# Cross attention of a streaming encoder step: half of the cached keys turned on VectorE, half on TensorE

## The chip, the cores and the metric

One Trainium2 chip, one core. The metric is device microseconds of one execution of the whole program. A profile is one execution more, recorded instruction by instruction, and times inside it count from the start of its span.

## What is computed

A two-layer encoder step. Each layer is a mixer, a cross attention and a SwiGLU, over 512 frames of one new stream (the prompt) and 16 frames of each of 8 running streams (the samples). Only the cross attention matters here:

```python
def cross_attn(h, mk, mv, w_q, w_o):
    b, t, _ = h.shape
    q = (h @ w_q).reshape(b, t, X_HEADS, X_HEAD_DIM)
    s = jnp.einsum('bqhd,bkhd->bhqk', q, mk).astype(jnp.float32) * X_SCALE
    p = jax.nn.softmax(s, axis=-1).astype(mv.dtype)
    o = jnp.einsum('bhqk,bkhd->bqhd', p, mv).reshape(b, t, X_WIDTH)
    return o @ w_o
```

There are 4 heads of 256 dimensions and 256 memory tokens. For the prompt, keys and values come from `mem_prompt` and were written to device memory earlier in the program (`kvd`). For the 8 samples they are inputs, `cache_mem_k` and `cache_mem_v` of shape (2, 8, 256, 4, 256).

## The kernel before

Every product with a weight is made of fp32 values split in two parts, hi and lo, and three passes (hi by hi, hi by lo, lo by hi). `load_w` fetches a weight in units of 1024 columns (`raw`, two buffers), and `split_unit` (L142) splits each: hi on ScalarE (L150), lo on VectorE (L151), three buffers of each part.

`cross_phase` runs once per layer. It first makes the queries of heads 0 and 1 (`q_list`, L840), then merges three lists of steps four times (L1035 to L1038): `sample_list(pr, bq)` for a pair of heads and four samples, `prompt_list(h)` for one head of the prompt, and either the queries of a later head or a part of the output projection. The merged stretches are called stages 1 to 4 here.

- `q_list`: per head four products of 320 columns (two halves `dt` of the head's 256 dimensions, two halves of the 640 frames), each 24 matmuls at L204 whose stationary side is 128 columns of the weight. Each `dt` has a weight unit of its own (all 8 blocks of 128 rows by 128 columns).
- `sample_list`: `keys` (L947) turns one key, the 256 by 256 block of one head of one sample: four transposes on TensorE into PSUM (L956), and one copy to `KT`, on VectorE for every second sample (L960, `b % 2 == 0`), on ScalarE for the others (L962). There are 32 keys a layer, 8 a stage. `load_key` asks for a key three keys ahead, one DMA of 256 KB into one of four `kr` buffers (L941). After 8 keys follow `scores` (L969), the softmax, `trans` (L978), `values` (L992, with `vr` from L985) and `turn` (L1002).
- `prompt_list`: `load` asks for the head's keys and values (`kv`, one buffer, L884), `keys` turns the keys (L891), then twice scores (L218), softmax, `trans` (L915) and values (L218).

The program's text is not yet the order of the work: a scheduler in the layer below puts the instructions of each engine in order, each engine then runs its own in that order, and they wait for each other by semaphores. All the DMAs here go through SP's one queue, in order.

The forgetting attention (`fox_phase`) already has the kind of step that the change brings: its cached keys are loaded by four DMAs of 32 partitions each (L684) and turned by VectorE in blocks of 32 by 32 (L692).

Of the kernel before, what the change touches and what calls it, by code (L numbers as in the profile page):

```python
# [9 lines left out]
F32 = mybir.dt.float32  # L10
# [8 lines left out]
P = 128  # L19
D = 1024  # L20
KD = D // P
# [71 lines left out]
def fox_mla_kernel(ctx: ExitStack, tc: tile.TileContext, I, O):  # L93
# [72 lines left out]
    def load_w(cols, k0=0, kt=KD, per=4):  # L166
        parts = []
        n = max(c1 for _, c1, _ in cols)
        k = 0
        while k < kt:  # L170
            m = min(per, kt - k)
            srcs = []
            for c0, c1, src in cols:
                sv = src[(k0 + k) * P:(k0 + k + m) * P, :].rearrange("(k p) n -> p k n", p=P)
                srcs.append((c0, c1, sv))
            hi, lo = split_unit(srcs, m, n)
            parts.append((m, hi, lo))
            k += m
        return Weight(parts)
# [3 lines left out]
    def ws_ops(w, wc, acts, ac, kt):  # L183
        return [(w.get(wi, k)[:, wc], acts[ai][:, k, ac]) for wi, ai in PASSES for k in range(kt)]
# [643 lines left out]

    def cross_phase(l, nx, rest):
        w_q, w_o = I["w_x_q"][l], I["w_x_o"][l]  # L830
        mk = I["cache_mem_k"][l].rearrange("b (m p) h d -> p (b m) (h d)", p=P)
        mv = I["cache_mem_v"][l].rearrange("b (m p) h d -> p (b m) (h d)", p=P)
        with tc.tile_pool(name=f"x{l}", bufs=2, reuse_waits="tile") as xp:
            AHEAD = 3
# [5 lines left out]
            def q_list(h):  # L840
                Q = Qps[h // 2]
                L = []
                d = {}

                def load(dt):
                    if dt == 0:
                        qs_[h] = [xp.tile([P, 2, NP], F32R, tag=f"qT{i}", name=f"qT{i}", bufs=2) for i in range(2)]
                    c0 = h * XD + dt * P
                    d[dt] = load_w([(0, P, w_q[:, c0:c0 + P])], per=8)

                def done(ps, dt, half):
                    qT = qs_[h]
                    n = HALF if half == 0 else NP - HALF
                    hs = slice(half * HALF, half * HALF + n)
                    evac_split(qT[0][:, dt, hs], qT[1][:, dt, hs], ps[:, 0:n], X_SCALE)
                    if half == 1:
                        o = TS * (h % 2)
                        A.activation(Q[:, 2 * (h % 2) + dt, :, o:o + TS],
                                     ps[:, n:HALF].rearrange("p (b t) -> p b t", t=TS), AF.Copy, scale=X_SCALE)

                for half in range(2):
                    for dt in range(2):
                        if half == 0:
                            L.append(lambda dt=dt: load(dt))
                        L += gemm(lambda dt=dt, half=half: ws_ops(d[dt], slice(0, P), nx.T,
                                                                  slice(half * HALF, (half + 1) * HALF), KD),
                                  HALF, lambda ps, dt=dt, half=half: done(ps, dt, half), parts=3)
                return L

            def softmax(pw, sp):  # L870
                nm = small.tile([P, 1], F32, tag="nm", name="nm")
# [2 lines left out]
                A.activation(pw, sp[:, 0:NMEM], AF.Exp, bias=nm, accum_out=ss)  # L874
                softmax_tail(pw, ss, NMEM)

            def prompt_list(h):
                d = {}

                def load():  # L880
                    kv = npool.tile([P, 2, 2, XD], F32, tag="gb", name="kv", bufs=1)
                    d["kv"] = [kv[:, i] for i in range(2)]
                    for i in range(2):
                        S.dma_start(kv[:, i], kvd[l][i].rearrange("(t p) n -> p t n", p=P)[:, :, h * XD:(h + 1) * XD])  # L884

                def keys():
                    d["kT"] = [xp.tile([P, 2, NMEM], F32R, tag=f"kT{i}", name=f"kT{i}", bufs=1) for i in range(2)]
                    pt = psum_t()
                    for dt in range(2):
                        for mt in range(2):  # L890
                            T.transpose(out=pt[:, dt * NMEM + mt * P:dt * NMEM + (mt + 1) * P],  # L891
                                        in_=d["kv"][0][:, mt, dt * P:(dt + 1) * P], identity=ident)
                    evac_split(d["kT"][0], d["kT"][1], pt.rearrange("p (d m) -> p d m", m=NMEM))
                    d["v"] = [xp.tile([P, 2, XD], F32R, tag=f"v{i}", name=f"v{i}", bufs=1) for i in range(2)]
                    evac_split(d["v"][0], d["v"][1], d["kv"][1])
                    oTp[h] = [xp.tile([P, 2, NP], F32R, tag=f"oT{i}", name=f"oT{i}", bufs=3) for i in range(2)]

                def scores(q2):
                    buf = npool.tile([P, D], F32, tag="hn", name="hn", bufs=2)
                    d["pw"] = [buf[:, j * NMEM:(j + 1) * NMEM] for j in range(2)]  # L900
                    for j in range(2):
                        qc = slice((2 * q2 + j) * P, (2 * q2 + j + 1) * P)
                        sp = psum_s()
                        for dt in range(2):
                            mm3(sp[:, 0:NMEM], [q[:, dt, qc] for q in qs_[h]], [k[:, dt, :] for k in d["kT"]],
                                start=(dt == 0), stop=(dt == 1))
                        softmax(d["pw"][j], sp)

                def trans():
                    d["PT"] = [xp.tile([P, 2, 256], F32R, tag=f"PT{i}", name=f"PT{i}", bufs=1) for i in range(2)]  # L910
                    pt = psum_t()
                    for mt in range(2):
                        for j in range(2):
                            i = 2 * mt + j
                            T.transpose(out=pt[:, i * P:(i + 1) * P], in_=d["pw"][j][:, mt * P:(mt + 1) * P],  # L915
                                        identity=ident)
                    evac_split(d["PT"][0], d["PT"][1], pt.rearrange("p (m q) -> p m q", q=256))

                def values(q2):
                    op = psum_o()  # L920
                    for dt in range(2):
                        for mt in range(2):
                            mm3(op[:, dt * 256:(dt + 1) * 256], [v[:, mt, dt * P:(dt + 1) * P] for v in d["v"]],
                                [p_[:, mt, :] for p_ in d["PT"]], start=(mt == 0), stop=(mt == 1))
                    oc = slice(q2 * 256, (q2 + 1) * 256)
                    evac_split(oTp[h][0][:, :, oc], oTp[h][1][:, :, oc], op.rearrange("p (d q) -> p d q", q=256))

                L = [load, keys]
                for q2 in range(2):
                    L += [lambda q2=q2: scores(q2), trans, lambda q2=q2: values(q2)]  # L930
                return L
# [3 lines left out]
            def load_key(n):  # L935

                if n < 32:
                    pr, bq, hh, b = n // 16, n // 8 % 2, n // 4 % 2, n % 4
                    hc = slice((2 * pr + hh) * XD, (2 * pr + hh + 1) * XD)
                    krs[n] = xp.tile([P, 2, XD], F32, tag="kr", name="kr", bufs=4)  # L940
                    S.dma_start(krs[n], mk[:, 2 * (4 * bq + b):2 * (4 * bq + b) + 2, hc])  # L941

            def sample_list(pr, bq):
                Q = Qps[pr]
# [2 lines left out]
                def keys(hh, b):  # L947
                    n = 16 * pr + 8 * bq + 4 * hh + b
                    load_key(n + AHEAD)
                    kr = krs.pop(n)  # L950
                    if b % 2 == 0:
                        d["KT"][hh, b // 2] = xp.tile([P, 2, 2, NMEM], F32, tag="KT", name="KT", bufs=4)
                    pt = psum_t()
                    for dt in range(2):
                        for mt in range(2):
                            T.transpose(out=pt[:, dt * NMEM + mt * P:dt * NMEM + (mt + 1) * P],  # L956
                                        in_=kr[:, mt, dt * P:(dt + 1) * P], identity=ident)
                    src = pt.rearrange("p (d m) -> p d m", m=NMEM)
                    if b % 2 == 0:
                        V.tensor_copy(d["KT"][hh, b // 2][:, 0], src)  # L960
                    else:
                        A.copy(d["KT"][hh, b // 2][:, 1], src)  # L962

                def scores():
                    sp = psum_s()
# [64 lines left out]
            for n in range(AHEAD):  # L1030
                load_key(n)
            ql = q_list(0)
            for f in ql[:6] + rest[:1] + ql[6:8] + rest[1:] + ql[8:] + q_list(1):
                f()
            merge(sample_list(0, 0), prompt_list(0), q_list(2))  # L1035
            merge(sample_list(0, 1), prompt_list(1), q_list(3))
            merge(sample_list(1, 0), prompt_list(2), out_steps(0))
# [757 lines left out]
```

## Time and profile before

| | us |
|---|---|
| median of 3 runs | 2092.14 |
| lowest and highest run | 2087.58, 2093.4 |
| the profiled execution, its own time | 2091.71 |
| its span in the trace | 2089.9 |
| mean granted clock of TensorE | 0.996 of full speed |

The span is the time from the first to the last instruction. "PE" is TensorE's matmuls, "PEld" its loads of the stationary side, which overlap matmuls; DVE is VectorE, ACT ScalarE, POOL GpSimd, SP the engine that issues the DMAs. L204 is line 204 of the kernel.

### The profile page before, as it was taken

How to read it: one execution, taken by the hardware profiler on the slowest of the kernel's cores; microseconds unless marked ns; L12 is line 12 of the kernel's file. 1: busy time of each engine (PE TensorE's matmuls, PEld its weight loads, DVE VectorE, ACT ScalarE, POOL GpSimd, SP SyncE). 2: the span in 40 equal slices, each digit the busy share in tenths (PEclk: the TensorE clock that was granted, in tenths of full speed). 3: DMA queues.
4: the chain of work that ended last, by engine and by line, in shares of the span. 5: the costliest groups of instructions: out<-in, count | busy, mean ns of one | idle time of the engine just before them, and what ended most of it. 6: DMA issues, size and time to landing. Idle time of an engine off the chain costs nothing. (4 is left out here: it accounts for less than half of the span.)

```text
span 2089.9 us, 34810 instructions
## 1 busy us (share of the span) xinstructions
PE 2034.7 (97%) x13629; PEld 1817.9 (87%) x13629; DVE 1390.8 (67%) x2658; ACT 888.0 (42%) x1723; POOL 195.2 (9%) x398
## 2 busy tenths in 40 slices
PE   7999999999999999999999989999999999999998
PEld 7988888777987899999998978887987899999996
DVE  5455555655556896687677567777556896686686
ACT  4434444544443443343344455554443443343342
POOL 1222222210000000000002301101000000000000
PEclk9999999999999999999999999999999999999999
DMA  7565655477464322232222342113463322232221
GB/s 194 119 160 124 148 135 142 146 243 229 151 197 133 100 88 74 81 91 71 81 82 64 96 109 52 53 51 102 149 196 131 101 81 75 80 99 71 81 81 61
DMA packets 334203, 236.37 MB, mean 113 GB/s; under 512 B 99140, under 2 KB 298564, under 8 KB 334040
## 3 DMA queue, kind: packets, MB, share of 16 engines
q1 hardware_dynamic: 334040, 234.15, 38.8%
q8 instruction: 108, 1.77, 0.4%
q14 instruction: 55, 0.45, 0.1%
HBM read 216.90 MB, written 17.21 MB: 112 GB/s over the span
## 5 line engine op out<-in xcount | busy, mean ns | idle before, releaser
L204 PE MATMUL mm<-hT,whi 128*128 128x320 f32 x1744 | 287.5, 311 | 2.9 <-ACT hT L222 2.9
L151 DVE TENSOR_TENSOR wlo<-raw,whi 128x1024 fp32r<-128x1024 f32 (+4 forms) x145 | 169.8, 1174 | 156.5 <-ACT whi L150 116.5
L204 PEld LDWEIGHTS mm<-hT,whi 128*128 128x128 f32 x1744 | 261.0, 188 | 6.8 <-ACT hT L222 4.3
L332 DVE TENSOR_TENSOR X<-mm,X 128x512 f32<-128x512 f32 x270 | 183.5, 687 | 119.7 <-PE mm L204 118.1
L150 ACT CAST whi<-raw 128x1024 fp32r<-128x1024 f32 (+4 forms) x145 | 144.8, 1003 | 146.7 <-PE mm L204 74.9
L204 PE MATMUL mm<-whi,oT 128*128 128x512 f32 x544 | 180.3, 407 | 3.8 <-DVE X L332 2.2
L1136 ACT CAST whi<-tw 128x512 fp32r<-128x512 f32 (+1 forms) x120 | 91.9, 766 | 213.7 <-PE mm L204 127.4
L204 PE MATMUL mm<-whi,aT 128*128 128x512 f32 x560 | 173.0, 390 | 1.2 <-ACT aT L1101 1.2
L204 PE MATMUL mm<-hT,wlo 128*128 128x320 f32 x872 | 156.7, 312 | 0.0
L204 PEld LDWEIGHTS mm<-hT,wlo 128*128 128x128 f32 x872 | 133.3, 188 | 3.3 <-issue 3.2
L232 POOL TENSOR_SCALAR rstd<-ss 128x1 f32<-128x1 f32 x49 | 16.2, 330 | 1265.4 <-ACT hn L230 1261.0
L204 PE MATMUL mm<-s,whi 128*128 128x320 f32 x768 | 128.2, 309 | 0.0
L204 PE MATMUL mm<-whi,hT 128*128 128x256 f32 (+2 forms) x800 | 125.5, 295 | 0.3 <-ACT whi L150 0.3
L204 PEld LDWEIGHTS mm<-whi,aT 128*128 128x128 f32 x560 | 104.4, 188 | 23.5 <-ACT aT L1101 2.0
L204 PEld LDWEIGHTS mm<-whi,oT 128*128 128x128 f32 x544 | 96.7, 189 | 26.2 <-DVE X L332 4.6
L204 PEld LDWEIGHTS mm<-s,whi 128*128 128x128 f32 x768 | 116.6, 188 | 0.0
L1137 DVE TENSOR_TENSOR wlo<-tw,whi 128x512 fp32r<-128x512 f32 (+1 forms) x120 | 103.5, 862 | 19.1 <-ACT whi L1136 17.4
L204 PEld LDWEIGHTS mm<-whi,hT 128*128 128x128 f32 x800 | 109.1, 191 | 3.8 <-issue 1.7
L204 PE MATMUL mm<-wlo,oT 128*128 128x512 f32 x272 | 109.0, 401 | 0.0
L204 PE MATMUL mm<-wlo,aT 128*128 128x512 f32 x280 | 108.8, 389 | 0.0
L1136 ACT CAST whi<-raw 128x1024 fp32r<-128x1024 f32 x44 | 46.3, 1052 | 131.7 <-PE mm L204 71.0
L204 PE MATMUL ps_s<-whi,aT 128*128 128x512 f32 x320 | 98.6, 389 | 0.0
(336 smaller groups left out, 4199.4 us busy)
## 6 DMA issues: line engine op xcount, KB each, us to landing
rawg<-w_ffn_gu SPq DMA_DIRECT2D x80, 512.0 KB, 3.8
raw<-w_ffn_down SPq DMA_DIRECT2D x44, 512.0 KB, 3.7
raw<-w_x_kv SPq DMA_DIRECT2D x32, 512.0 KB, 4.4
kr<-cache_mem_k SPq DMA_DIRECT2D x64, 256.0 KB, 4.8
vr<-cache_mem_v SPq DMA_DIRECT2D x32, 512.0 KB, 6.1
raw<-w_fox_in SPq DMA_DIRECT2D x30, 512.0 KB, 6.5
kr<-cache_fox_k SPq DMA_DIRECT2D x64, 128.0 KB, 5.1
vr<-cache_fox_v SPq DMA_DIRECT2D x16, 512.0 KB, 5.2
```

The source lines that it names most:

```text
L150: A.copy(hi[:, 0:m], raw[:, 0:m])
L151: V.tensor_tensor(lo[:, 0:m], raw[:, 0:m], hi[:, 0:m].bitcast(F32), ALU.subtract)
L204: T.matmul(st["ps"][:, 0:n], lhsT=l, rhs=r, start=(j == 0), stop=(j == m - 1))
L232: G.tensor_scalar(r, ss, EPS, None, ALU.add)
L332: V.tensor_tensor(xs, ps, xs, ALU.add)
L1136: A.copy(hi[:, o:o + m], src)
L1137: V.tensor_tensor(lo[:, o:o + m], src, hi[:, o:o + m].bitcast(F32), ALU.subtract)
```

## The change

For every second sample (`b % 2 == 0`, 16 keys a layer) the key is loaded as 32 partitions by 8 by 64 numbers, by four DMAs of 64 KB in runs of 256 bytes, and `V.transpose` turns it in blocks of 32 by 32 straight into `KT`; the four transposes on TensorE and VectorE's copy out of PSUM go. In this layout the two halves of a head's dimensions are the even and the odd ones. So the other keys' transposes, those of the prompt's keys and the query product take every second column as the stationary side, and a head's query weight comes in two units of 4 blocks by 256 columns, both asked for ahead of the head's first product. `load_kv` asks for the prompt's keys and values of a head right behind the turning of the head before.

```diff
     def cross_phase(l, nx, rest):
...
-        mk = I["cache_mem_k"][l].rearrange("b (m p) h d -> p (b m) (h d)", p=P)
+        mkp = I["cache_mem_k"][l].rearrange("b (m p) h d -> p (b m) (h d)", p=P)
+        mk = I["cache_mem_k"][l].rearrange("b (m j) h d -> b j m (h d)", j=32)
...
-                def load(dt):
...
-                    c0 = h * XD + dt * P
-                    d[dt] = load_w([(0, P, w_q[:, c0:c0 + P])], per=8)
+                def load():
+                    qs_[h] = [xp.tile([P, 2, NP], F32R, tag=f"qT{i}", name=f"qT{i}", bufs=2) for i in range(2)]
+                    d["w"] = load_w([(0, XD, w_q[:, h * XD:(h + 1) * XD])])
+
+                def ops(dt, half):
+
+                    hs = slice(half * HALF, (half + 1) * HALF)
+                    return [(d["w"].get(wi, k).rearrange("p (n t) -> p t n", t=2)[:, dt], nx.T[ai][:, k, hs])
+                            for wi, ai in PASSES for k in range(KD)]
...
+            def fill_keys(r, src, h):
+
+                for g in range(4):
+                    c0 = h * XD + 64 * g
+                    S.dma_start(r[32 * g:32 * g + 32], src[:, :, c0:c0 + 64])
+
+            def turn_keys(dst, r):
+                V.transpose(dst, r.rearrange("p m (i t) -> p t m i", t=2))
...
             def prompt_list(h):
...
                 def keys():
+                    d["kv"] = kvs.pop(h)
...
-                                        in_=d["kv"][0][:, mt, dt * P:(dt + 1) * P], identity=ident)
+                                        in_=d["kv"][0][:, mt].rearrange("p (n t) -> p t n", t=2)[:, dt], identity=ident)
...
-                L = [load, keys]
+                L = [keys, lambda: load_kv(h + 1)]
...
-                    krs[n] = xp.tile([P, 2, XD], F32, tag="kr", name="kr", bufs=4)
-                    S.dma_start(krs[n], mk[:, 2 * (4 * bq + b):2 * (4 * bq + b) + 2, hc])
+                    if b % 2 == 0:
+                        krs[n] = xp.tile([P, 8, 64], F32, tag="kr", name="kr", bufs=4)
+                        fill_keys(krs[n], mk[4 * bq + b], 2 * pr + hh)
+                    else:
+                        hc = slice((2 * pr + hh) * XD, (2 * pr + hh + 1) * XD)
+                        krs[n] = xp.tile([P, 2, XD], F32, tag="kr", name="kr", bufs=4)
+                        S.dma_start(krs[n], mkp[:, 2 * (4 * bq + b):2 * (4 * bq + b) + 2, hc])
...
                     if b % 2 == 0:
                         d["KT"][hh, b // 2] = xp.tile([P, 2, 2, NMEM], F32, tag="KT", name="KT", bufs=4)
+                        turn_keys(d["KT"][hh, b // 2][:, 0], kr)
+                        return
                     pt = psum_t()
...
-                                        in_=kr[:, mt, dt * P:(dt + 1) * P], identity=ident)
-                    src = pt.rearrange("p (d m) -> p d m", m=NMEM)
-                    if b % 2 == 0:
-                        V.tensor_copy(d["KT"][hh, b // 2][:, 0], src)
-                    else:
-                        A.copy(d["KT"][hh, b // 2][:, 1], src)
+                                        in_=kr[:, mt].rearrange("p (n t) -> p t n", t=2)[:, dt], identity=ident)
+                    A.copy(d["KT"][hh, b // 2][:, 1], pt.rearrange("p (d m) -> p d m", m=NMEM))
...
+            load_kv(0)
             merge(sample_list(0, 0), prompt_list(0), q_list(2))
```

The scheduler then orders the engines anew. TensorE at the start of stage 1 of the first layer before (kr and kv are raw keys, hT the activations, whi and wlo the weight's parts):

```order
L204 MATMUL mm<-hT_6091,wlo 128x320 x4
L956 MATMUL ps_t<-cst,kr 128x128 x8
L204 MATMUL mm<-hT_6090,whi 128x320 x4
L204 MATMUL mm<-hT_6091,whi 128x320 x4
L956 MATMUL ps_t<-cst,kr 128x128 x4
L204 MATMUL mm<-hT_6092,whi 128x320 x4
```

and with the change (L906 turns the prompt's keys, L977 the samples'):

```order
L204 MATMUL mm<-hT_6091,wlo 128x320 x4
L906 MATMUL ps_t<-cst,kv 128x128 x4
L977 MATMUL ps_t<-cst,kr 128x128 x4
L204 MATMUL mm<-hT_6090,whi 128x320 x4
L204 MATMUL mm<-hT_6091,whi 128x320 x4
L204 MATMUL mm<-hT_6092,whi 128x320 x4
```

Two of the three keys that stood here are gone, and the prompt's keys stand first. TensorE behind the samples' scores of stage 1 before (pws is the softmax's result, PTs its transpose, vr the cached values):

```order
L969 MATMUL ps_s<-KT,Qp_6193 32x256 x16
L915 MATMUL ps_t<-cst,hn 128x128 x4
L204 MATMUL mm<-hT_6090,whi 128x320 x4
L204 MATMUL mm<-hT_6091,whi 128x320 x4
L204 MATMUL mm<-hT_6092,whi 128x320 x4
L204 MATMUL mm<-hT_6093,whi 128x320
L978 MATMUL ps_t<-cst,pws 128x128 x2
L204 MATMUL mm<-hT_6093,whi 128x320 x3
L204 MATMUL mm<-hT_6090,wlo 128x320
L992 MATMUL ps_o<-vr,PTs 32x256 x16
```

and with the change:

```order
L986 MATMUL ps_s<-KT,Qp_6193 32x256 x16
L204 MATMUL mm<-hT_6090,whi 128x320 x4
L204 MATMUL mm<-hT_6091,whi 128x320 x4
L930 MATMUL ps_t<-cst,hn 128x128 x4
L204 MATMUL mm<-hT_6092,whi 128x320
L995 MATMUL ps_t<-cst,pws 128x128 x2
L204 MATMUL mm<-hT_6092,whi 128x320 x3
L204 MATMUL mm<-hT_6093,whi 128x320 x4
L1009 MATMUL ps_o<-vr,PTs 32x256 x10
```

Between scores and the transpose of their softmax there stood 13 matmuls of 320 columns, and now 9; behind it 4, and now 7. SP's queue for stage 2 of the first layer before:

```order
L941 DMA kr<-cache_mem_k 128x2x256 x4
L884 DMA kv<-kvd_85 128x2x256 x2
L941 DMA kr<-cache_mem_k 128x2x256 x3
L148 DMA raw<-w_x_o 128x1024
L985 DMA vr<-cache_mem_v 128x4x256 x3
L941 DMA kr<-cache_mem_k 128x2x256
L985 DMA vr<-cache_mem_v 128x4x256
```

and with the change:

```order
L895 DMA kv<-kvd_85 128x2x256 x2
L876 DMA kr<-cache_mem_k 32x8x64 x4
L960 DMA kr<-cache_mem_k 128x2x256
L1002 DMA vr<-cache_mem_v 128x4x256
L876 DMA kr<-cache_mem_k 32x8x64 x4
L1002 DMA vr<-cache_mem_v 128x4x256
L960 DMA kr<-cache_mem_k 128x2x256
L1002 DMA vr<-cache_mem_v 128x4x256
L876 DMA kr<-cache_mem_k 32x8x64 x4
L1002 DMA vr<-cache_mem_v 128x4x256
L960 DMA kr<-cache_mem_k 128x2x256
L148 DMA raw<-w_x_o 128x1024 x2
```

Before, a stage's four DMAs of values stood together at the end of the stage ahead (the rows above hold stage 3's). Now they stand one by one among the keys of their own stage, the last of them behind four DMAs for a key of the next stage.

## Rows read from the trace of the kernel before

**Rows 1.** The page's head: the span, and busy time of each engine.
```profile
span 2089.9 us, 34810 instructions
...
PE 2034.7 (97%) x13629; PEld 1817.9 (87%) x13629; DVE 1390.8 (67%) x2658; ACT 888.0 (42%) x1723; POOL 195.2 (9%) x398
```
**Rows 2.** Busy time by stretch: stages 1 to 4, first and second layer.
```profile
core 0: us, PE busy (x) PEld busy (x) DVE busy (x) ACT busy (x) POOL busy (x), PEclk, DMA share, GB/s
557.50:676.00 118.50, 118.07 (x938) 99.47 (x940) 68.15 (x141) 49.52 (x114) 0.00 (x0) 1.00 0.52 168
1500.00:1615.00 115.00, 113.95 (x894) 95.71 (x893) 64.55 (x137) 46.16 (x108) 0.00 (x0) 1.00 0.52 169
```
**Rows 3.** Groups by line: loads of the keys' transposes; busy, mean ns | idle before.
```profile
L956 PEld LDWEIGHTS ps_t<-cst,kr 128*128 128x128 f32 x256 | 30.0, 140 | 6.1 <-DMA kr<-cache_mem_k 2.2 <-ACT KT L962 1.6 <-DVE KT L960 0.4
...
L891 PEld LDWEIGHTS ps_t<-cst,kv 128*128 128x128 f32 x32 | 3.5, 141 | 1.7 <-ACT KT L962 1.7
```
**Rows 4.** Timeline of TensorE's loads in stage 1: start, us, what.
```profile
572.85 0.51 PEld L956 LDWEIGHTS ps_t<-cst,kr 128*128 128x128 f32 x4
573.32 1.17 PEld L204 LDWEIGHTS mm<-hT,whi 128*128 128x128 f32 x8
```
**Rows 5.** Timeline of TensorE's loads ahead of stage 1, query product of head 1.
```profile
552.97 1.22 PEld L204 LDWEIGHTS mm<-hT,wlo 128*128 128x128 f32 x8
554.14 2.39 PEld L204 LDWEIGHTS mm<-hT,whi 128*128 128x128 f32 x16
556.49 1.21 PEld L204 LDWEIGHTS mm<-hT,wlo 128*128 128x128 f32 x8
```
**Rows 6.** Groups by line: VectorE's copy of a key, and its block transpose.
```profile
L960 DVE COPY KT<-ps_t 128x512 f32<-128x512 f32 x32 | 22.0, 688 | 8.1 <-PE ps_t L956 8.1
L692 DVE STREAM_TRANSPOSE KT<-kr 128x512 f32<-128x512 f32 x32 | 21.6, 693 | 0.0
```
**Rows 7.** The page's DMA issues: KB each, median us from issue to landing.
```profile
kr<-cache_mem_k SPq DMA_DIRECT2D x64, 256.0 KB, 4.8
vr<-cache_mem_v SPq DMA_DIRECT2D x32, 512.0 KB, 6.1
...
kr<-cache_fox_k SPq DMA_DIRECT2D x64, 128.0 KB, 5.1
```
**Rows 8.** Two lines' issues on SP: ns of one issue, least, median, most.
```profile
L941 SPq DMA_DIRECT2D kr<-cache_mem_k x64: 367/368/679, 515.2 to 1594.9; - x64
...
L684 SPq DMA_DIRECT2D kr<-cache_fox_k x64: 321/562/3513, 18.0 to 357.1; - x64
```
**Rows 9.** Timeline at the first layer's first query product.
```profile
527.29 2.64 PEld L204 LDWEIGHTS mm<-hT,whi 128*128 128x128 f32 x18 [1.05 <-ACT hT L222]
...
529.21 1.22 DVE L151 TENSOR_TENSOR wlo<-raw,whi 128x1024 fp32r<-128x1024 f32 x1
```
**Rows 10.** Timeline of TensorE's loads from the samples' scores to values, stage 1.
```profile
577.30 1.45 PEld L969 LDWEIGHTS ps_s<-KT,Qp 128*32 128x32 f32 x32 [0.19 <-issue]
579.16 0.42 PEld L915 LDWEIGHTS ps_t<-cst,hn 128*128 128x128 f32 x4 [0.41 <-issue]
579.55 1.92 PEld L204 LDWEIGHTS mm<-hT,whi 128*128 128x128 f32 x13
581.79 0.20 PEld L978 LDWEIGHTS ps_t<-cst,pws 128*128 128x128 f32 x2 [0.33 <-issue]
...
582.75 0.81 PEld L992 LDWEIGHTS ps_o<-vr,PTs 128*32 128x32 f32 x20 [0.19 <-ACT PTs L980]
```
**Rows 11.** Loads for matmuls of 16 columns, L457: timeline's ends, and the counts.
```profile
51.87 0.30 PEld L457 LDWEIGHTS ps_t<-pw,cst 128*128 128x128 f32 x2
...
54.10 0.45 PEld L204 LDWEIGHTS mm<-hT,wlo 128*128 128x128 f32 x3
...
L457 PEld LDWEIGHTS ps_t<-pw,ones x12: 192/192/192, 52.1 to 53.8; 128*128 128x128 f32 x12
...
L457 PEld LDWEIGHTS ps_t<-pw,cst x8: 186/192/192, 51.9 to 54.0; 128*128 128x128 f32 x8
```

More of the change, by code (lines that the diff above doesn't have):

```diff
@@ L843, in q_list @@
                 d = {}
-                def load(dt):
-                    if dt == 0:
-                        qs_[h] = [xp.tile([P, 2, NP], F32R, tag=f"qT{i}", name=f"qT{i}", bufs=2) for i in range(2)]
-                    c0 = h * XD + dt * P
-                    d[dt] = load_w([(0, P, w_q[:, c0:c0 + P])], per=8)
+                def load():
[5 more added lines that the diff above has]
+                            for wi, ai in PASSES for k in range(KD)]
                 def done(ps, dt, half):
@@ L862, in q_list @@
                     for dt in range(2):
[L863 to L868, printed above, removed]
+                        L += gemm(lambda dt=dt, half=half: ops(dt, half), HALF,
+                                  lambda ps, dt=dt, half=half: done(ps, dt, half), parts=3)
+                return [load] + L
+            def fill_keys(r, src, h):
[4 more added lines that the diff above has]
+                V.transpose(dst, r.rearrange("p m (i t) -> p t m i", t=2))
             def softmax(pw, sp):
@@ L875, in softmax, with load_kv @@
                 softmax_tail(pw, ss, NMEM)
+            kvs = {}
+            def load_kv(h):
+                if h < 4:
+                    kv = npool.tile([P, 2, 2, XD], F32, tag="gb", name="kv", bufs=1)
+                    kvs[h] = [kv[:, i] for i in range(2)]
+                    for i in range(2):
+                        S.dma_start(kv[:, i], kvd[l][i].rearrange("(t p) n -> p t n", p=P)[:, :, h * XD:(h + 1) * XD])
             def prompt_list(h):
                 d = {}
[L880 to L884, printed above, removed]
                 def keys():
+                    d["kv"] = kvs.pop(h)
                     d["kT"] = [xp.tile([P, 2, NMEM], F32R, tag=f"kT{i}", name=f"kT{i}", bufs=1) for i in range(2)]
@@ L938, in load_key @@
                     pr, bq, hh, b = n // 16, n // 8 % 2, n // 4 % 2, n % 4
-                    hc = slice((2 * pr + hh) * XD, (2 * pr + hh + 1) * XD)
-                    krs[n] = xp.tile([P, 2, XD], F32, tag="kr", name="kr", bufs=4)
-                    S.dma_start(krs[n], mk[:, 2 * (4 * bq + b):2 * (4 * bq + b) + 2, hc])
+                    if b % 2 == 0:
[5 more added lines that the diff above has]
+                        S.dma_start(krs[n], mkp[:, 2 * (4 * bq + b):2 * (4 * bq + b) + 2, hc])
             def sample_list(pr, bq):
@@ L1032, in cross_phase @@
             ql = q_list(0)
-            for f in ql[:6] + rest[:1] + ql[6:8] + rest[1:] + ql[8:] + q_list(1):
+            for f in ql[:5] + rest[:1] + ql[5:7] + rest[1:] + ql[7:] + q_list(1):
                 f()
+            load_kv(0)
             merge(sample_list(0, 0), prompt_list(0), q_list(2))
```

## The prediction

> **What bounds the kernel now.** I read the page's head first. TensorE's matmuls are busy 97% of the span, VectorE 67%, ScalarE 42% [rows 1]: this is a TensorE kernel, and a change pays by what it takes out of TensorE's own sequence. The change sits in stages 1 to 4 of the two cross attentions, so I read those stretches next. There TensorE is busy 118.07 of 118.50 us and 113.95 of 115.00 us, at the full granted clock, so 1.5 us of idle time is all that waits cost there. VectorE is busy 68 of 118 and 65 of 115 us [rows 2]. So what is to be seen is a TensorE without gaps, and beside it a VectorE with four tenths of its time free. The keys' transposes wait little: 6.1 us on their loads in 64 keys, most of it under running matmuls [rows 3].
>
> **Transposes that go.** Half of the keys leave TensorE: 16 in each layer, 32 in all, four transposes each. One such group holds the sequence from 572.85 to 573.32 us, where the next load stands, 0.47 us [rows 4]. 32 by 0.47 is 15.0 us, all of it on the engine that bounds, at a place without gaps.
>
> **VectorE.** 32 copies of 688 ns become 32 block transposes; the same kind of instruction at the same size takes 693 ns in the first phase [rows 6]: 0.2 us more in all. That one reads its input in order, the new one every second number. No row has that step on VectorE, so the bounds are nothing and twice 693 ns, 22 us more on an engine with some 100 us free in the two stretches [rows 2]. I take nothing: the copy was read out of PSUM behind TensorE, the transpose needs only the key, which was asked for three keys ahead, so it can stand early. ScalarE's part is as before.
>
> **DMAs.** 32 keys come by four DMAs instead of one, 96 issues more. An issue took 368 ns for whole keys, 562 ns for the quarter keys of the first phase [rows 8], so SP works some 128 by 0.56 less 32 by 0.37, 60 us more, 7.5 us in a stage of about 29 us, and has room. The landing of a whole key took 4.8 us; the nearest rows to the new DMAs, 32 partitions each in runs of 128 bytes, landed in 5.1 us [rows 7]. I take 5.1 us and no wait for keys, with the price of being wrong in the second rival. The query weight keeps its 16 units, in longer runs. The prompt's keys one head ahead I cost at nothing: their transposes waited 1.7 us, all of it for ScalarE's copies and none for the load [rows 3]. What it could cost: `kv` has one buffer, so this DMA holds SP until the head's keys are turned and split, and the samples' keys queue behind it.
>
> **New order.** Two gaps grow. Behind the samples' scores of stages 1 and 2 TensorE has 2.63 us to fill until the softmax is there (579.16 to 581.79 us); it has 13 matmuls and four transposes for it and still waits 0.33 us [rows 10]. A query matmul takes 147 ns (24 loads from 552.97 to 556.49 us [rows 5]). With 9 matmuls in that place the gap is 4 by 0.147, 0.59 us longer; the three more behind the softmax's transposes close the 0.19 us wait there. Net 0.4 us in each of two stages and layers, 1.6 us; in stage 3 less work stands behind the transposes too, an estimate of 0.4 us a layer, 0.8 us. The other is the first query product: it now needs the second unit's lo after 20 matmuls, at 527.29 + 20 by 0.147, 530.23 us, and VectorE's split ended at 530.43 us [rows 9]: 0.2 us a layer, 0.4 us. Against it, of the 1.5 us of idle time I let 0.5 us go with the removed transposes.
>
> **Strided stationary side.** 768 query matmuls (8 products of heads by 4 by 24) and 160 remaining transposes load every second column. No row shows such a load. The lower bound is nothing: columns in order are the fastest reading seen. The upper bound is a load at half the rate. Where the moving side is only 16 columns, loads alone set the pace: 20 of them from 51.87 to 54.10 us, 111 ns each [rows 11]. That is well under the 147 ns of a query matmul, so the load is hidden with 36 ns to spare, and I take nothing. By "SBUF — State Buffer" (section "Door 1: The DMA port swizzle", its note on cachelines) of the Trainium skill, an SBUF line is 16 bytes, and two reads out of one line already go at full rate; every second fp32 number still gives two per line, so by that page the price is nothing too. No run here shows it yet.
>
> **The sum.** -15.0 - 0.5 + 1.6 + 0.8 + 0.4 = -12.7 us. The profiled execution took 2091.71 us, 0.4 us below the median of the three runs, so I predict **2079 us**, own range 2072 us (all waits in the stretches gone as well, and the spread of runs) to 2085 us (half the gain lost in new gaps).
>
> **First rival, slower: the strided loads.** Place: the query products. If such a load ran at half rate, 223 ns, a query matmul would take 223 instead of 147 ns, 768 by 0.076 = 58 us, and 160 transposes 0.111 us more each, 18 us: 2079 + 76 = 2155 us. It decides against the change from the point where 768 by (111 f - 147) and 160 by 111 (f - 1) ns eat 12.7 us, f = 1.39, a load each 155 ns. For it: nothing in the profile shows the stride free. Against it: the stride needs no more than twice the line reads, and loads had room. Chance 0.12. The same note of "SBUF — State Buffer" in the Trainium skill also says that each access that crosses to a new line pays; with the stride every second access does, which read strictly is this rival.
>
> **Second rival, no change: new waits take the gain.** In stage 2 the last DMA of values stands behind four for key 18, which wait for the buffer of key 14, that is for VectorE's turn of it, placed amid the prompt's second scores. From there the chain is 0.69 + 4 by 0.56 + 6.1 us, 9.0 us [rows 6 to 8]. TensorE has for it 8 matmuls and a key's transposes, 1.6 us, the way from scores to values, 5.45 us [rows 10], some 8 matmuls amid the values, 1.2 us, and half of the prompt's scores, under 1 us: about 9 us as well. So it is even, and each contention of DMAs shows. At 2 us a stage, in stages 2 to 4 of both layers, 12 us are lost: 2091 us. For it: the DMAs' share of 0.52 [rows 2] with five issues where two were for each pair of keys. Against it: buffers free before TensorE arrives. Chance 0.17, from 2085 to 2098 us. "DMA: Bandwidth & Descriptors" (Specifications) of the Trainium skill asks for at least 512 bytes a run for the full rate and says that shorter ones cost a read-modify-write; the new keys come in 256 byte runs, and landings twice as long would bring this rival about. The rows with 128 byte runs (5.1 against 4.8 us) don't bear that out.
>
> **Third, more gain:** under 2072 us, if half-empty gaps close that I don't see. Chance 0.04.
>
> **Chances.** The forecast has 0.67. About 0.3% (6 us) is what a measurement of this kernel can tell from no change, so faster means under 2085.4 us: forecast and third case, 0.71. Same is the second rival, 0.17, and slower the first, 0.12. The range 2072 to 2095 us leaves out the first rival, the third case, and the upper end of the second, 0.19 together.
>
> **What would show it.** 128 matmuls fewer on TensorE, and in stages 1 to 4 some 6 to 7 us less per layer at the same lack of gaps. Right: query matmuls still 147 ns apart, block transposes near 0.69 us, no wait named by `kr` or `vr` over 1 us in total. Wrong: query loads over 155 ns apart (first rival); TensorE waiting for `vr` at values or VectorE for `kr`, and from VectorE's lateness TensorE at the softmax's transposes (second). The gaps behind the samples' scores should read about 0.9 us instead of 0.33.

## The result and the profile after

The changed kernel took 2078.72 us (median of 4 runs, 2077.78 to 2079.67). The kernel before, now with a fourth run of 2088.70 us, stood at 2090.42 us. The ratio is 0.9939, 95% interval 0.9925 to 0.9954: 11.7 us less, faster by 0.6%. Run once more beside the last experiments it took 2078.20 us against 2092.93 us, ratio 0.9927 [0.9915, 0.9940].

The head of the page after, against [rows 1]:

```profile
span 2076.5 us, 34659 instructions
...
PE 2022.2 (97%) x13501; PEld 1809.6 (87%) x13501; DVE 1390.2 (67%) x2658; ACT 884.8 (43%) x1723; POOL 196.9 (9%) x398
```

128 matmuls fewer, TensorE busy 12.5 us less, span 13.4 us less, and VectorE as busy as before: its turns are as long as the copies that they replace. Busy time by stretch, each cross attention from the first copy of a query product to the start of the last product with `oTs`, before:

```profile
core 0: us, PE busy (x) PEld busy (x) DVE busy (x) ACT busy (x) POOL busy (x), PEclk, DMA share, GB/s
531.50:707.30 175.80, 175.14 (x1277) 150.74 (x1276) 101.74 (x189) 69.26 (x149) 2.38 (x6) 1.00 0.49 154
1471.30:1648.30 177.00, 175.72 (x1278) 150.89 (x1277) 101.69 (x189) 69.33 (x149) 2.37 (x6) 1.00 0.46 145
```

and after:

```profile
530.10:702.00 171.90, 169.36 (x1213) 146.12 (x1212) 101.54 (x189) 67.69 (x149) 2.37 (x6) 1.00 0.58 162
1463.40:1633.80 170.40, 168.52 (x1216) 146.13 (x1215) 101.43 (x189) 67.79 (x149) 2.37 (x6) 1.00 0.56 160
```

The cross attentions went from 352.8 to 342.3 us: 10.5 us of the span's 13.4. TensorE's busy time there fell by 13.0 us, and its idle time rose from 1.9 to 4.4 us. So the transposes' gain came, and a part of it was lost again in new gaps. The groups by line show where not to look:

```profile
L879 DVE STREAM_TRANSPOSE KT<-kr 128x512 f32<-128x512 f32 x32 | 22.5, 702 | 0.6 <-DMA kr<-cache_mem_k 0.6
...
L977 PEld LDWEIGHTS ps_t<-cst,kr 128*128 128x128 f32 x128 | 18.7, 204 | 0.8
```

A turn on VectorE takes 702 ns and waited once for a key, 0.6 us. The strided loads last 204 instead of 140 ns [rows 3], but they stand in nobody's way: no idle time of note before them. The DMA issues of the page agree (KB each, median us to landing):

```profile
vr<-cache_mem_v SPq DMA_DIRECT2D x32, 512.0 KB, 5.5
...
kr<-cache_mem_k SPq DMA_DIRECT2D x128, 64.0 KB, 4.1
kr<-cache_mem_k SPq DMA_DIRECT2D x32, 256.0 KB, 2.7
```

The quarter keys land in 4.1 us, sooner than the 5.1 us that the prediction took, and nothing on TensorE waits for `kr` or `vr`. The timeline of TensorE's loads in stage 1, from the samples' scores on, shows where to look (start, us, what, and in brackets the idle time before):

```profile
574.27 1.45 PEld L986 LDWEIGHTS ps_s<-KT,Qp 128*32 128x32 f32 x32 [0.19 <-issue]
576.13 1.19 PEld L204 LDWEIGHTS mm<-hT,whi 128*128 128x128 f32 x8 [0.41 <-DVE KT L879]
577.28 0.50 PEld L930 LDWEIGHTS ps_t<-cst,hn 128*128 128x128 f32 x4
577.75 0.20 PEld L204 LDWEIGHTS mm<-hT,whi 128*128 128x128 f32 x1
578.00 0.20 PEld L995 LDWEIGHTS ps_t<-cst,pws 128*128 128x128 f32 x2
578.17 1.05 PEld L204 LDWEIGHTS mm<-hT,whi 128*128 128x128 f32 x7
579.41 1.01 PEld L1009 LDWEIGHTS ps_o<-vr,PTs 128*32 128x32 f32 x20 [0.19 <-issue]
580.83 1.20 PEld L204 LDWEIGHTS mm<-hT,wlo 128*128 128x128 f32 x8 [0.41 <-issue]
582.22 0.58 PEld L1009 LDWEIGHTS ps_o<-vr,PTs 128*32 128x32 f32 x12 [0.18 <-issue]
583.96 1.13 PEld L218 LDWEIGHTS ps_o<-PT,v 128*128 128x128 f32 x9 [1.17 <-ACT osb L1014]
```

and from the samples' values on before (L992 are the samples' values, L218 the prompt's):

```profile
582.75 1.45 PEld L992 LDWEIGHTS ps_o<-vr,PTs 128*32 128x32 f32 x32 [0.19 <-ACT PTs L980]
584.62 0.73 PEld L204 LDWEIGHTS mm<-hT,wlo 128*128 128x128 f32 x5 [0.41 <-issue]
585.42 1.49 PEld L218 LDWEIGHTS ps_o<-PT,v 128*128 128x128 f32 x12
```

In the changed kernel TensorE has no wait ahead of the softmax's transposes, although less work stands there. The new ones are behind it. The samples' values (L1009) come in two pieces, and each piece costs a step of 0.19 us into the narrow loads and of 0.41 us out of them; before they were one piece in every stage, and now they are two in three of the eight. And the prompt's values (L218) stand straight behind them and wait: there is one `o` buffer in PSUM, and ScalarE must first copy the samples' values out of it (`osb`). Before, five matmuls of query products or four of the output product stood between. Who waited for `osb` in the changed kernel:

```profile
  PEld ps_o L218: 5.9, 5
  PE ps_o L218: 3.5, 5
```

Five of eight stages have this wait. The main groups of TensorE's loads taken together (each from its start to the start of the next, in the first and second cross attention, so a wait counts with the group ahead of it), in us:

| loads for | before | after |
|---|---|---|
| the samples' keys (L956, L977) | 15.4 + 15.3 | 8.3 + 8.3 |
| the samples' values (L992, L1009) | 7.5 + 7.5 | 10.8 + 9.1 |
| query products | 53.7 + 54.2 | 53.2 + 53.3 |
| output products | 55.9 + 56.4 | 55.2 + 55.2 |
| the prompt's scores, values, keys | 25.1 + 25.7 | 26.3 + 26.4 |

The keys gave 14.2 us, output and query products 3.2 us, the values took back 5.0 us, the prompt's part 1.9 us. The groups left out changed by 0.1 us in all.

### The profile page after: what moved, and what is told of

Read it like the earlier page. It is cut to its first block, busy times and chain, and to the rows that moved or that the text cites. A ratio compares the mean times of both kernels' runs of the same rounds, so it can differ in the third digit from the quotient of the medians.

```text
span 2076.5 us, 34659 instructions
## 1 busy us (share of the span) xinstructions
PE 2022.2 (97%) x13501; PEld 1809.6 (87%) x13501; DVE 1390.2 (67%) x2658; ACT 884.8 (43%) x1723; POOL 196.9 (9%) x398
## 3 DMA queue, kind: packets, MB, share of 16 engines
q1 hardware_dynamic: 351960, 234.16, 40.4%
## 5 line engine op out<-in xcount | busy, mean ns | idle before, releaser
L151 DVE TENSOR_TENSOR wlo<-raw,whi 128x1024 fp32r<-128x1024 f32 (+4 forms) x145 | 170.0, 1175 | 136.0 <-ACT whi L150 115.7
```

The costliest lines, as they stand in the source:

```text
L151: V.tensor_tensor(lo[:, 0:m], raw[:, 0:m], hi[:, 0:m].bitcast(F32), ALU.subtract)
```

## The experiments

Each was set against the kernel before on its own chip. e1 to e4 ran on one chip, e5 to e8 and, at another time, the last four rows on a second. "Over" and "under the changed kernel" set a median against 2078.72 us, for the last rows against the 2078.20 us beside them.

| | median us | ratio to before, 95% |
|---|---|---|
| e1 all but VectorE's turns | 2094.81 | 1.0015 [1.0001, 1.0029] |
| e2 prompt's keys late | 2077.61 | 0.9929 [0.9915, 0.9943] |
| e3 transposes put back | 2098.61 | 1.0032 [1.0021, 1.0043] |
| e4 runs of 128 bytes | 2086.93 | 0.9978 [0.9966, 0.9989] |
| e5 all keys on VectorE | 2127.94 | 1.0170 [1.0157, 1.0184] |
| e6 osb in halves | 2077.16 | 0.9924 [0.9912, 0.9937] |
| e7 values in the s ring | 2081.37 | 0.9949 [0.9936, 0.9961] |
| e8 values asked for early | 2115.31 | 1.0113 [1.0098, 1.0129] |
| the changed kernel again | 2078.20 | 0.9927 [0.9915, 0.9940] |
| e9 no stride | 2076.59 | 0.9920 [0.9906, 0.9933] |
| e11 three of four keys | 2103.60 | 1.0046 [1.0033, 1.0060] |
| e12 e2 and e6 together | 2078.13 | 0.9924 [0.9911, 0.9936] |

### What the transposes were worth: e1, e3

e1 keeps all of the change but VectorE's turns; every key comes whole and goes through TensorE.

```diff
-                    if b % 2 == 0:
-                        krs[n] = xp.tile([P, 8, 64], F32, tag="kr", name="kr", bufs=4)
-                        fill_keys(krs[n], mk[4 * bq + b], 2 * pr + hh)
...
-                        turn_keys(d["KT"][hh, b // 2][:, 0], kr)
-                        return
...
+                    if b % 2 == 0:
+                        V.tensor_copy(d["KT"][hh, b // 2][:, 0], src)
...
```

> All keys on TensorE again, the rest of the change kept (stride-2 stationary sides, the query weight as one load of two units, prompt keys one head ahead). Theory A, the gain is the transposes that left TensorE, and the stride is hidden: no change against the kernel before, 2087 to 2093 us, query loads 147 ns apart. Theory B, the strided loads cost something that the gain covers: over 2095 us. Theory C, a part of the gain comes from the new way of loading the query weight and the prompt's keys: 2081 to 2086 us.

It came out between A and B, 3.7 us over the kernel before, just clear of no difference. Theory C falls: nothing of the gain is in the rest of the change. The rest costs something, and e9 shows how much of it is the stride; in e1 TensorE also waits 2.5 us for keys in the second layer (0.7 us there before).

e3 leaves the changed kernel as it is and adds the removed transposes, their result unread.

```diff
                         turn_keys(d["KT"][hh, b // 2][:, 0], kr)
+                        pt = psum_t()
+                        for i in range(4):
+                            T.transpose(out=pt[:, i * P:(i + 1) * P], in_=kr.rearrange("p m c -> p (m c)")[:, i * P:(i + 1) * P], identity=ident)
                         return
```

> The changed kernel with four TensorE transposes of each VectorE-turned key put back, their result unread. Theory A, each group costs TensorE its 0.47 us in a sequence without gaps: 32 by 0.47, 15 us more than the changed kernel, 2091 to 2096 us. Theory D, the new gaps (some 2 us of idle time in each stretch of stages) take part of them up: 4 to 10 us more, 2083 to 2089 us.

It took 19.9 us more than the changed kernel, over A's range, and D falls: the new gaps do not take such work up. The loads' sequence gives 16.5 us to the added groups, 0.52 us each. Of the rest, 2.2 us are the samples' scores in the new order: 67 instead of 58 ns a load.

### The smaller parts: e2, e9, e4

e2 asks for the prompt's keys at their own head again:

```diff
-                L = [keys, lambda: load_kv(h + 1)]
+                L = [lambda: load_kv(h), keys]
...
-            load_kv(0)
```

> The changed kernel with the prompt's keys asked for at their own head's start, as before the change. Theory A, asking one head ahead is worth nothing, since the load was hidden: 2076 to 2082 us, under 0.15% from the changed kernel. Theory C, it is a part of the gain: 2083 to 2088 us, with TensorE's prompt transposes waiting for kv.

A holds: 1.1 us under the changed kernel, within the spread. Asking one head ahead is worth nothing.

e9 reads the stationary sides in order, with the same instructions in the same order on every engine:

```diff
-                    return [(d["w"].get(wi, k).rearrange("p (n t) -> p t n", t=2)[:, dt], nx.T[ai][:, k, hs])
+                    return [(d["w"].get(wi, k)[:, dt * P:(dt + 1) * P], nx.T[ai][:, k, hs])
...
-                                        in_=kr[:, mt].rearrange("p (n t) -> p t n", t=2)[:, dt], identity=ident)
+                                        in_=kr[:, mt, dt * P:(dt + 1) * P], identity=ident)
```

(The prompt's keys are read in order in the same way.)

> The changed kernel, instruction for instruction in the same order, with TensorE's three strided stationary sides (query weight, remaining keys, prompt's keys) read in order instead of every second column. It computes something else: the halves of the keys that VectorE turned no longer belong to the queries' halves. Theory A, the stride is hidden at the query products and costs the 160 transposes a few ns each: 0 to 2 us less than the changed kernel. Theory B, it costs some of the 3 us that lay between the strided kernel without VectorE's turns and the kernel before: 3 to 5 us less.

A holds: 1.6 us under the changed kernel on the same chip. The groups by line:

```profile
L977 PEld LDWEIGHTS ps_t<-cst,kr 128*128 128x128 f32 x128 | 15.5, 140 | 1.4
```

In order, a load takes 140 ns; with the stride 204 ns (above). Yet in the loads' sequence the samples' keys shrink from 16.5 to 15.6 us only, 7 ns a load, and both cross attentions together by 1.5 us. Nearly all of the longer load lies under the matmul ahead of it.

e4 reads the columns in order, with e9's edits and a turn that fits, and pays with runs of 128 bytes and eight DMAs a key:

```diff
-                    c0 = h * XD + 64 * g
-                    S.dma_start(r[32 * g:32 * g + 32], src[:, :, c0:c0 + 64])
+                    for t in range(2):
+                        c0 = h * XD + P * t + 32 * g
+                        S.dma_start(r[32 * g:32 * g + 32, :, 32 * t:32 * t + 32], src[:, :, c0:c0 + 32])
...
```

> The changed kernel with the columns in order (no stride on TensorE) and therefore keys in runs of 128 bytes, eight DMAs for a key instead of four. Theory A, stride and runs are both hidden: within 3 us of the changed kernel, 2076 to 2082 us, transposes' groups 0.47 instead of 0.49 us. Theory B, the stride costs: under 2075 us. Theory E, the shorter runs and the 128 more issues come late: over 2083 us, with VectorE's turns waiting for kr or TensorE for vr.

E holds by its time, 8.2 us over the changed kernel, and by a wait for `vr`. The samples' values in its groups by line, TensorE first, then the loads:

```profile
L1010 PE MATMUL ps_o<-vr,PTs 128*32 128x256 f32 x256 | 18.2, 384 | 2.1 <-DMA vr<-cache_mem_v 1.7 <-ACT PTs L998 0.4
...
L1010 PEld LDWEIGHTS ps_o<-vr,PTs 128*32 128x32 f32 x256 | 7.9, 109 | 9.8 <-DMA vr<-cache_mem_v 2.8 <-issue 1.9 <-ACT PTs L998 1.1
```

Here TensorE waits for `vr`, once and 1.7 us long; `vr` stands in SP's queue behind the doubled issues. The larger part is the output product's weight, which stands in the same queue: its split on ScalarE waits 8.8 us for `raw<-w_x_o` in the two cross attentions, and TensorE waits 4.9 us for its parts `whi` and `wlo`. The changed kernel has none of these waits there. A part of a key lands in 2.8 us and no longer; it is the queue that is late. The stride costs 1.5 us and buys four issues a key instead of eight; without it, with twice the issues, the kernel is 8.2 us slower.

### The new gaps: e6, e7, e8, e12

```diff
-                    A.copy(d["osb"], op)
+                    A.copy(d["osb"][:, 0:256], op[:, 0:256])
+                    V.tensor_copy(d["osb"][:, 256:512], op[:, 256:512])
```

> The changed kernel with the copy of the samples' values out of PSUM (osb) split between ScalarE and VectorE, 256 columns each, so that PSUM's one o buffer comes free sooner. Theory F, TensorE's new idle time is the wait for that copy (0.7 us in five of eight stages): half of it goes, 1 to 3 us less than the changed kernel, 2076 to 2078 us. Theory H, the idle time only moves to another wait: no change, 2078 to 2081 us.

```diff
-                    op = psum_o()
+                    op = psum_s()
```

> The changed kernel with the samples' values in PSUM's s ring (two buffers) instead of the one o buffer, so that the prompt's values no longer wait for osb. Theory F: the 0.7 to 0.9 us in five stages go, 3 to 5 us less than the changed kernel, 2073.5 to 2076 us, no wait named osb. Theory H, the scores that share the ring wait instead: no change or slower, 2078 to 2083 us.

e6 reads 1.6 us under the changed kernel, in F's range, but within the spread. And it does not test F, since its halves do not run side by side. Stage 1 of e6:

```profile
584.55 0.37 ACT L1014 COPY osb<-ps_o 128x256 f32<-128x256 f32 x1
584.95 0.43 DVE L1015 COPY osb<-ps_o 128x256 f32<-128x256 f32 x1 [0.68 <-ACT osb L1014]
584.97 0.20 PEld L1020 LDWEIGHTS ps_t<-cst,osb 128*128 128x128 f32 x2 [0.95 <-ACT osb L1014]
```

In all eight stages VectorE's half begins only after ScalarE's has ended. The two together take 0.83 us where the one copy took 0.59 us, so the buffer comes free no sooner, and in five stages TensorE still waits, now 0.95 to 0.97 us ahead of `turn` (L1020).

e7 is 2.7 us over the changed kernel, and F falls there. Who waited for `osb` in e7:

```profile
  PEld ps_t L1019: 5.1, 5
  PE ps_t L1019: 2.9, 5
```

The prompt's values no longer wait, but now `turn` (L1019) stands behind the samples' values and waits for the same copy, again five times. And there are more pieces of values than before, fourteen instead of eleven, with the same 0.41 us out of each that no wait for `osb` follows. By these five waits the copy is not short of a buffer, it is short of work placed beside it.

> The changed kernel with the prompt's keys asked for at their own head (as in the run before) and osb's copy in two halves. Each alone read 1 to 2 us under the changed kernel, within the spread. If both are real: 2074 to 2076.5 us. If both are spread: 2077 to 2080 us.

e12, with both edits, reads 2078.13 us beside 2078.20 us of the changed kernel: e2's and e6's one to two us do not add up to a gain. For e6 the trace says a little more than the median: its cross attentions take 340.7 us, against 342.3 us in both traces of the changed kernel. In e12's order they take 342.7 us.

```diff
-                    if i >= 4:
-                        L.append(lambda i=i: load_v(i % 4 // 2, i % 2))
+                    if 2 <= i < 6:
+                        L.append(lambda i=i: load_v((i - 2) // 2, i % 2))
```

> The changed kernel with the samples' values (vr) asked for two keys sooner, which lets the order keep their 32 matmuls in one piece. Theory F, pieces and the wait for osb cost the part of the gain that did not come: 1 to 3 us less in the two first stages of each layer, 2074 to 2078 us. Theory H, the order changes but TensorE's idle time stays: 2078 to 2082 us.

Both theories fall. The values did come in one piece in seven of eight stages, and the kernel lost 37 us, the cross attentions alone 33.7 us (376.0 against 342.3). Of these, 20.5 us are idle time and 13.2 us longer busy time of TensorE. The scheduler put the last of the samples' scores right ahead of the transposes of their softmax in stages 3 and 4, and TensorE waits there, over both layers, 7.2 us for the softmax (`pws`) and 2.8 us for VectorE's turns. The rest of the loss is not taken apart here. That the values' DMAs, now ahead of the keys' in SP's queue, are what moved the scores is argued from the order and was not tried by itself.

### More of the same: e5, e11

e5 turns all keys on VectorE, e11 three of four (`b != 3`). e11's edit:

```diff
-                    if b % 2 == 0:
+                    if b != 3:
                         krs[n] = xp.tile([P, 8, 64], F32, tag="kr", name="kr", bufs=4)
...
-                        turn_keys(d["KT"][hh, b // 2][:, 0], kr)
+                    if b != 3:
+                        turn_keys(d["KT"][hh, b // 2][:, b % 2], kr)
```

> The other half of the keys is turned by VectorE too: 128 more transposes leave TensorE, 32 copies leave ScalarE, VectorE gets 32 turns of 0.70 us, SP 96 more DMAs. Theory A, TensorE's sequence still bounds, and what the first half was worth against its own put-back (between 15 and 20 us) comes again: 2060 to 2066 us. Theory G, VectorE and SP are used up (64 turns, 256 DMAs with runs of 256 bytes): turns wait for kr, TensorE for KT at the samples' scores, and the gain is under 4 us, 2075 to 2085 us.

> Three of four keys turned by VectorE instead of two (64 more transposes off TensorE, 16 turns and 48 DMAs more). Theory A with a cliff only near all keys: 32 groups were worth 16 us, 16 more are worth 8, 2068 to 2073 us. Theory G, the chain that ended the run with all keys (a turn frees a key buffer, four issues and the landing follow, the next turn stands late in VectorE's queue) already binds: over 2080 us, TensorE waiting for KT at the samples' scores.

For e5 both theories fall, G by its size (49 us over the changed kernel) and, as shown below, by VectorE being used up; that TensorE waits for `KT` at the scores came true. e11 is 25.4 us over the changed kernel, as G has it, but not by G's sign: over both layers TensorE's matmuls wait 0.4 us for `KT` at the samples' scores, 9.8 us for the softmax and 5.6 us for `osb`. The timeline of TensorE's matmuls in e11, stage 2:

```profile
603.46 1.49 PE L987 MATMUL ps_s<-KT,Qp 128*32 128x256 f32 x20
...
608.32 0.62 PE L987 MATMUL ps_s<-KT,Qp 128*32 128x256 f32 x2
...
610.44 1.05 PE L987 MATMUL ps_s<-KT,Qp 128*32 128x256 f32 x10
613.29 0.41 PE L996 MATMUL ps_t<-cst,pws 128*128 128x128 f32 x2 [1.79 <-DVE pws L345]
614.16 3.09 PE L1010 MATMUL ps_o<-vr,PTs 128*32 128x256 f32 x32 [0.46 <-ACT PTs L998]
617.93 2.93 PE L218 MATMUL ps_o<-PT,v 128*128 128x256 f32 x12 [0.69 <-ACT osb L1015]
```

The scores come in three pieces, and all work that could stand behind them is used up ahead of the last. Softmax, transposes and values then follow each other with nothing between. The last group is suddenly longer: 2.93 us for the twelve of L218, 1.69 us in stage 1 of the changed kernel. The same time by stretch, with the granted clock behind POOL's column:

```profile
608.00:612.00 4.00, 3.41 (x25) 1.91 (x23) 1.09 (x3) 1.32 (x4) 0.00 (x0) 1.00 0.71 221
612.00:616.00 4.00, 2.25 (x26) 1.27 (x30) 2.54 (x6) 1.09 (x4) 0.00 (x0) 0.85 0.90 288
616.00:620.00 4.00, 3.31 (x21) 2.29 (x14) 1.15 (x1) 1.53 (x2) 0.00 (x0) 0.50 0.45 98
620.00:624.00 4.00, 4.00 (x22) 3.66 (x21) 2.58 (x5) 2.93 (x6) 0.00 (x0) 0.80 0.15 43
624.00:628.00 4.00, 4.00 (x27) 3.63 (x26) 3.79 (x9) 1.72 (x5) 0.00 (x0) 1.00 0.80 212
```

From 608 to 616 us TensorE is busy 5.66 of 8 us. Towards the end of this stretch the clock falls (0.85); from 616 to 620 us it stands at 0.50 of full speed, 1.2 GHz, and it is back at 2.4 GHz by 624 us. Both cross attentions of e11 ran at a mean clock of 0.97: TensorE busy 349.0 us against 337.9 us, with 64 transposes fewer. So of the 26.0 us that e11's cross attentions are longer (368.3 against 342.3), 11 us are busy time and 15 us idle time, 19.3 against 4.4 us. The missing 0.03 of the clock over 368.3 us is 11 us as well, an estimate; but busy time should have fallen with the transposes that went, and what made up for that was not separated. In e5 the clock is 0.97 too, and TensorE waits 11.3 us for VectorE's turns and 14.3 us for the softmax.

VectorE is not used up there: 221.7 of 394.4 us in e5. That the turns are late is argued from the chain: SP waits 33.8 us from 530 to 690 us in e5 for a turn to free a `kr` buffer (18.0 us in the changed kernel), four issues and a landing follow, and the next turn stands in VectorE's order behind work that waits for ScalarE. More `kr` buffers would test this; it was not tried.

## Why the prediction was right, and where not

The prediction was 2079 us with a range of 2072 to 2095 us; 2078.72 us was measured, and the sum of -12.7 us stands between the medians' 11.7 and the span's 13.4 us. In the cross attentions, to which the sum belongs, only 10.5 us came, 3.9 us in the first layer and 6.6 us in the second, where the prediction had 6 to 7 us in each and no more idle time than before. Point by point:

- **Transposes that go, -15.0.** Right: 14.2 us less in the loads' sequence. Put back they cost 16.5 us as groups, and 16 to 20 us with all that they brought along (e1 and e3 over the changed kernel). TensorE's sequence is the bound.
- **Relieved waits, -0.5.** Too small, by the same sequence: before, loads of keys waited 4.2 us in the groups ahead of them, most of it behind output products, and none do now. The 3.2 us less in the products may well be these waits; that was not tried by itself.
- **VectorE, 0.** Right: 702 against 688 ns, and turns that wait 0.6 us in all. But the margin was not the 100 us of free time that the step names: with 8 turns more in each layer (e11) it is gone.
- **DMAs, 0.** Right, and the quarter keys landed in 4.1 us. Its price if wrong, the second rival, is what e4 ran into: there the queue is late. "DMA: Bandwidth & Descriptors" (Specifications) of the Trainium skill, with its read-modify-write below 512 bytes, would have let landings grow. The pieces in runs of 256 and 128 bytes landed in 4.1 and 2.8 us, no later than a whole key before (4.8 us), but they are a quarter and an eighth of its bytes, and whole keys now land in 2.7 us. By the pages of the profile the same 234 MB took 40.4% of the DMA engines' span instead of 38.8%. So a price of short runs is not ruled out; it did not reach TensorE.
- **Strided stationary side, 0.** Nearly: 1.5 us (e9), against 76 us of the first rival. Query loads are still 147 ns apart (16 loads from 552.74 to 555.09 us). The load itself does last longer, 204 against 140 ns. By "SBUF — State Buffer" ("Door 1: The DMA port swizzle") of the Trainium skill, two reads out of one line give full rate; the trace agrees on the price, which is near nothing, and not on the load's own time.
- **Gap behind the samples' scores, +1.6 and +0.8.** This step failed. It held the time from scores to softmax fixed at 4.49 us [rows 10] and took the work out of it. The softmax was not fixed: before, VectorE's reduction stood behind a weight's split (579.57 us, after 1.22 us of L151), and its scaling behind the split of the prompt's PT. In the new order the scores start at 574.27 us, the reduction stands at 576.27 us, and the transposes follow at 578.00 us, 3.73 us, without a wait. Stage 2 and the second layer read alike. In stage 3 the 0.39 us ahead of the transposes stay, and ahead of the values there are 0.54 instead of 0.37 us: 0.17 us a layer where the prediction had 0.4 us.
- **First query product, +0.4.** It did not come: the loads run on from 525.86 to 532 us without idle time. The step counted 20 matmuls ahead of the second unit's lo, 16 of hi and four of lo, but the row that it read has 18 of hi [rows 9]. With 22, that lo is needed at 529.06 us, and VectorE's split ended at 528.99 us; at the old times that is 527.29 + 22 by 0.147, 530.52 us, against 530.43 us.
- **Missing from the sum, +5.0.** The samples' values in pieces, and the wait for `osb` behind them: five stages with 1.17 instead of 0.41 us before the next load are 3.8 us, the step of 0.41 us out of a second piece in three stages 1.2 us. The order printed with the change already ends in a first piece (L1009 x10 of 16 rows), and the prediction read only the rows ahead of it. The 1.9 us more in the prompt's part were not foreseen either.
- **Outside the cross attentions, -2.9 of the span.** Open. Between the two cross attentions no instruction of TensorE's order changed, yet the way from the last product of the first to the first query copy of the second took 763.9 us before, 761.4 us after and 761.0 us in its second run; other kernels of the study show from 761.1 us (e12) to 765.8 us (e3). The time ahead of the first cross attention (1.4 us less after) and behind the second (1.2 us more) about cancel. TensorE's named waits there add up to 17.2 us before and 16.0 us after, so they tell about half of it; the other half is busy time (746.1 and 744.8 us).

So the mechanism and the price of the transposes were right, but that the total was met so closely is partly luck, by errors that offset each other: 2.8 us of gaps that (but for 0.3 us) did not come and some 3 us more from relieved waits and products on the one side, 5.0 and 1.9 us that were not foreseen on the other, and some 3 us outside.

## What to carry to other kernels

Moving work off the bounding engine pays its price only while the new order leaves that engine work for each wait. Here two of four keys are worth 12 us, and a third costs 25 us with VectorE only 58% busy. When a scheduler reorders, read the new order at each place where a single buffer changes hands: the gain leaks there, and the copy out of it needs other work beside it, since another buffer alone only moves the wait (e7).

## Not expected of the hardware

- A stationary side of every second fp32 column loads in 204 instead of 140 ns, and costs 7 ns a load in a sequence of transposes, nothing that shows at query products 147 ns apart.
- In the sequence of TensorE's loads, the change from 128-column loads to 32-column ones and back leaves 0.19 us before (0.36 us in stages 3 and 4) and 0.41 us after, whatever the profile names as its end, mostly nothing. The matmuls' records overlap these gaps.
- In e11 the clock fell to 0.50 for some 7 us of a stage, in a kernel whose mean clock still reads 0.992: its price is seen only by stretch.
